# Split GELU times gate: tile 0 in one piece, the last tile in its own input buffer

## The chip, the cores and the metric

The kernel runs on one core of a Trainium2 chip. The metric is the device time of one execution in microseconds (us). The engines that matter here are ScalarE (ACT in the profile), VectorE (DVE), SyncE (SP, which here only issues transfers and waits) and the core's 16 DMA engines. ACTq and SPq are the queues in which ACT and SP hand over transfers; the DMA queues that serve them are q10 (ACT) and q1 (SP).

## The reference

The input x is 32 x 512 x 2048 in float32, that is 16,384 rows of 2048 numbers, 134.2 MB. The output has 16,384 rows of 1024 numbers, 67.1 MB.

```python
x1, x2 = x[..., :1024], x[..., 1024:]
out = 0.5 * x1 * (1 + erf(x1 / sqrt(2))) * x2
```

## The kernel before

The rows are cut into 16 tiles. A tile has 128 partitions with R = 8 rows each: 64 KB per partition come in (8.39 MB a tile) and 32 KB go out (4.19 MB). Tile i uses the input buffer x_bufs[i % 2] and the output buffer o_bufs[i % 2], k = i % 2.

For each tile ACT computes the GELU of the first half of each row into the output buffer (L87), and DVE multiplies that buffer, in place, by the second half of each row (L95). A middle tile is worked in two pieces, of 5 and 3 rows (128x5120 and 128x3072 elements). The first and the last tile are worked in three pieces, of 2, 2 and 4 rows.

The order is written out by hand with semaphores. gelu_done counts the pieces of ACT for DVE, and mul_done the pieces of DVE for the queues. One semaphore per buffer pair, ready[k], counts both the loads into x_bufs[k] and the stores out of o_bufs[k]; ACT waits for its full count before a tile's first piece, so a tile begins when its own load and the store of two tiles earlier have both landed. DVE has no wait of its own except that for ACT.

- Loads are issued by SP (L49). Tile 0 is loaded in two halves of 4 rows, each with a semaphore of its own (first[0], first[1]), and tile 1 in one transfer; all three are issued at the start. Load i + 2 is issued when the products of tile i are done.
- Stores are issued by ACT (L56) for tiles 0 to 13, one transfer a tile, except that tile 0 is stored in two halves. ACT waits for the products of a tile, issues its store, and only then goes on to the next tile. Stores of tile 14 and of the two halves of tile 15 are issued by SP, with the semaphore tail_stored, for which SP waits at the very end (L125).
- A transfer of 4 KB, the opening, is issued by ACT at the start, into a scrap tile that nothing reads.

Of the kernel before, what the change touches and what calls it, by code (L numbers as in the profile page):

```python
# [1 line left out]

# [4 lines left out]

GELU = mybir.ActivationFunctionType.Gelu


@with_exitstack
def kernel(
    ctx: ExitStack,
    tc: tile.TileContext,
    x: bass.AP,
    out: bass.AP,
):
    nc = tc.nc
    P = nc.NUM_PARTITIONS

    x_flat = x.flatten_outer_dims()
    out_flat = out.flatten_outer_dims()
    n_rows, dim = x_flat.shape
    half = dim // 2

    R = 8
    x_t = x_flat.rearrange("(n p r) d -> n p r d", p=P, r=R)
    o_t = out_flat.rearrange("(n p r) d -> n p r d", p=P, r=R)
    n_tiles = x_t.shape[0]
    x_bufs = [nc.alloc_sbuf_tensor(f"x{k}_tile", [P, R, dim], x.dtype) for k in range(2)]  # L30
    o_bufs = [nc.alloc_sbuf_tensor(f"o{k}_tile", [P, R, half], out.dtype) for k in range(2)]

    first = [nc.alloc_semaphore(f"first{j}") for j in range(2)]
    ready = [nc.alloc_semaphore(f"ready{k}") for k in range(2)]
    gelu_done = nc.alloc_semaphore("gelu_done")
    mul_done = nc.alloc_semaphore("mul_done")
    tail_stored = nc.alloc_semaphore("tail_stored")
    opened = nc.alloc_semaphore("opened")  # L40
    scrap = nc.alloc_sbuf_tensor("scrap_tile", [8, 128], x.dtype)
    n = {sem.name: 0 for sem in [*first, *ready, gelu_done, mul_done, tail_stored, opened]}

    def counted(ins, sem, by):
        ins.then_inc(sem, by)
        n[sem.name] += by

    def load(i, rows, sem):
        ins = nc.sync.dma_start(out=x_bufs[i % 2][:, rows, :], in_=x_t[i][:, rows, :])  # L49
        counted(ins, sem, 16)  # L50
        return ins

    def store(queue, i, rows, sem):
        queue.wait_ge(mul_done, n[mul_done.name])
        counted(
            queue.dma_start(out=o_t[i][:, rows, :], in_=o_bufs[i % 2][:, rows, :]), sem, 16  # L56
        )

    opening = nc.scalar.dma_start(out=scrap[:, :], in_=x_t[0][:8, 0, :128])
    counted(opening, opened, 16)
    for ins in (
        opening,
        load(0, slice(0, 4), first[0]),
        load(0, slice(4, 8), first[1]),
        load(1, slice(0, 8), ready[1]),
    ):  # L70
        tc.no_tile_sem_insts.add(ins.ins.name)
    tc.close()
    tc.compile()  # L73

    for i in range(n_tiles):
        k = i % 2
        last = i == n_tiles - 1
        pieces = i == 0 or last
        steps = ((0, 2), (2, 4), (4, 8)) if pieces else ((0, 5), (5, 8))
        for lo, hi in steps:  # L80
            rows = slice(lo, hi)
            if i == 0 and lo % 4 == 0:
                nc.scalar.wait_ge(first[lo // 4], 16)
            elif lo == 0:
                nc.scalar.wait_ge(ready[k], n[ready[k].name])
            counted(
                nc.scalar.activation(  # L87
                    out=o_bufs[k][:, rows, :], in_=x_bufs[k][:, rows, :half], func=GELU
                ),
                gelu_done,  # L90
                1,
            )
            nc.vector.wait_ge(gelu_done, n[gelu_done.name])
            counted(
                nc.vector.tensor_mul(  # L95
                    out=o_bufs[k][:, rows, :],
                    in0=o_bufs[k][:, rows, :],
                    in1=x_bufs[k][:, rows, half:],
                ),
                mul_done,  # L100
                1,
            )
            if pieces and hi % 4 == 0:
                if last:
                    store(nc.sync, i, slice(hi - 4, hi), tail_stored)
                else:
                    store(nc.scalar, i, slice(hi - 4, hi), ready[k])
        if not pieces:
            if i == n_tiles - 2:
                store(nc.sync, i, slice(0, R), tail_stored)  # L110
            else:
                store(nc.scalar, i, slice(0, R), ready[k])
        if i + 2 < n_tiles:
            nc.sync.wait_ge(mul_done, n[mul_done.name])
            load(i + 2, slice(0, R), ready[k])


    nc.scalar.wait_ge(opened, 16)
    nc.scalar.drain()  # L119
    for sem in (*first, *ready, opened):  # L120
        nc.scalar.sem_clear(sem)
    nc.vector.drain()
    nc.vector.sem_clear(gelu_done)
    nc.sync.sem_clear(mul_done)
    nc.sync.wait_ge(tail_stored, n[tail_stored.name]).then_inc(  # L125
        tail_stored, -n[tail_stored.name]
    )


# [1 line left out]
_INS = ['x']  # L131
_OUTS = [((32, 512, 1024), 'float32')]


# [23 lines left out]
```

## Time and profile before

| What | Value |
|---|---|
| Median of 3 timed runs | 469.32 us (469.19 to 469.43) |
| Span of the profiled execution | 467.8 us; its own device time isn't listed apart from this span |
| DVE busy | 140.5 us (30%), 34 instructions |
| ACT busy | 115.5 us (25%), 35 instructions |
| ACT waiting for stores to land | 301.8 us, 14 times, 21.9 us at most |
| ACT waiting for loads to land | 35.6 us, 3 times |
| DVE waiting for ACT | 319.7 us, 18 times |
| SP's queue waiting for DVE, ahead of loads | 396.5 us, 14 times |
| q1 (SP's transfers) | 2880 packets, 142.61 MB, 70.6% of 16 engines' time |
| q10 (ACT's transfers) | 2176 packets, 58.73 MB, 29.1% |
| A load, hand-over to landing | 44.4 us (median) |
| A full store, hand-over to landing | 44.7 us (median) |

The span goes from the first to the last instruction of the execution. Busy shares are those of an engine over the span; the share of a DMA queue is the time that its packets took, over the time of 16 engines. A stretch of the span can show a DMA share a little over 1.00, because a packet is counted where it starts. A packet here is one run of contiguous bytes in a partition: 64 KB for a whole load, 32 KB for half a load or a whole store, 16 KB for half a store.

### The profile page before, as it was taken

What the parts mean: (1) busy time and instruction counts of PE and PEld (TensorE: products, weight loads), DVE (VectorE), ACT (ScalarE), POOL (GpSimd) and SP (SyncE); (2) the same over time, 40 slices, a digit from 0 to 9 for tenths busy, and PEclk for the clock granted to TensorE, in tenths of its full rate; (3) what the DMA queues carried; (4) which work ended last, traced back from release to release, by engine and by line L of the source; (5) the groups of instructions that cost most, each with busy time, mean ns of one, the idle gap of its engine ahead of it and who ended that gap; (6) DMA issues with size and microseconds to landing.
All of it is one profiled execution on the core that took longest, in us unless ns stands there. A gap on an engine that the chain in (4) does not pass through costs nothing.

```text
span 467.8 us, 154 instructions
## 1 busy us (share of the span) xinstructions
DVE 140.5 (30%) x34; ACT 115.5 (25%) x35; POOL 0.2 (0%) x4
## 2 busy tenths in 40 slices
DVE  0330515207051060511606115060150702507043
ACT  1320606041060410604105050050501506014060
POOL 0000000000000000000000000000000000000000
DMA  8999999999999999999999999999999999999988
GB/s 359 448 448 448 398 406 496 403 403 448 459 437 403 440 412 493 403 403 448 487 409 403 445 406 493 403 403 448 493 403 403 448 426 471 403 426 426 493 384 379
DMA packets 5057, 201.34 MB, mean 430 GB/s; under 512 B 568, under 2 KB 576, under 8 KB 576
## 3 DMA queue, kind: packets, MB, share of 16 engines
q1 hardware_dynamic: 2880, 142.61, 70.6%
q10 hardware_dynamic: 2176, 58.73, 29.1%
q14 instruction: 1, 0.01, 0.0%
HBM read 134.22 MB, written 67.11 MB: 430 GB/s over the span
## 4 chain that ended last, share of the span: by engine, by line
DMA 76%; DVE 14%; ACT 8%; ACTq 0%; SPq 0%; issue 0%
DMA out_dram<-o_tile 66%; DVE o_tile L95 14%; DMA x_tile<-in_x_dram 10%; ACT o_tile L87 8%; ACTq L119 0%; SPq L49 0%
## 5 line engine op out<-in xcount | busy, mean ns | idle before, releaser
L95 DVE TENSOR_TENSOR o_tile<-o_tile,x_tile 128x5120 f32<-128x5120 f32 (+3 forms) x34 | 140.5, 4171 | 319.7 <-ACT o_tile L87 319.7
L87 ACT ACTIVATE o_tile<-x_tile 128x5120 f32<-128x5120 f32 (+3 forms) x34 | 114.3, 3407 | 337.3 <-DMA out_dram<-o_tile 301.8
L87 ACT ACT_TABLE_LOAD x1 | 1.3, 1283 | 2.9 <-PEq L73 2.9
L142 POOL MEMSET const-bfloat16-1.0<- 128x1 bf16 x1 | 0.1, 102 | 0.0
L142 POOL MEMSET const-uint8-127<- 128x1 uint8 x1 | 0.1, 101 | 0.0
L142 POOL MEMSET const-float32-0.0<- 128x1 f32 x1 | 0.1, 99 | 0.2 <-issue 0.2
L142 POOL MEMSET const-float32-1.0<- 128x1 f32 x1 | 0.1, 98 | 0.0
## 6 DMA issues: line engine op xcount, KB each, us to landing
out_dram<-o_tile ACTq DMA_DIRECT2D x13, 4096.0 KB, 44.7
x_tile<-in_x_dram SPq DMA_DIRECT2D x2, 4096.0 KB, 16.7
out_dram<-o_tile ACTq DMA_DIRECT2D x2, 2048.0 KB, 34.4
out_dram<-o_tile SPq DMA_DIRECT2D x1, 4096.0 KB, 25.2
out_dram<-o_tile SPq DMA_DIRECT2D x2, 2048.0 KB, 7.8
x_tile<-in_x_dram SPq DMA_DIRECT2D x15, 44.4
scrap_tile<-in_x_dram ACTq DMA_DIRECT2D x1, 4.0 KB
```

Source lines behind the costliest of these rows:

```text
L87: nc.scalar.activation(out=o_bufs[k][:, rows, :], in_=x_bufs[k][:, rows, :half], func=GELU),
L95: nc.vector.tensor_mul(out=o_bufs[k][:, rows, :], in0=o_bufs[k][:, rows, :], in1=x_bufs[k][:, rows, half:],),
L142: nc = _bacc.Bacc("TRN2", target_bir_lowering=False, num_devices=1)
```

## The change

- **Tile 0** is loaded by one transfer with ready[0], worked in two pieces of 5 and 3 rows like the middle tiles, and stored by one transfer. The semaphores first[0] and first[1] are gone, and with them two clears at the end.
- **Tile 15** (the last) no longer uses an output buffer. ACT writes the GELU over the first half of each row in the input buffer. DVE writes the product into the front of the same buffer, packed: row r of the product lies at elements 1024 r to 1024 r + 1023 of each partition. A piece's product thus covers space that an earlier piece has read, and DVE now waits for its own earlier product (mul_done) before each of the three pieces. The two stores of tile 15 read from there, again 16 KB per partition each.
- **Store 13** counts on tail_stored and no longer on ready[1], so that ACT begins tile 15 when load 15 has landed.
- In the program text the load of tile i + 2 now stands ahead of the store of tile i. They are issued by different engines, and the order of instructions on each engine is otherwise the same.

```diff
-    def load(i, rows, sem):
-        ins = nc.sync.dma_start(out=x_bufs[i % 2][:, rows, :], in_=x_t[i][:, rows, :])
-        counted(ins, sem, 16)
+    def load(i):
+        ins = nc.sync.dma_start(out=x_bufs[i % 2][:, :, :], in_=x_t[i])
+        counted(ins, ready[i % 2], 16)
...
-        load(0, slice(0, 4), first[0]),
-        load(0, slice(4, 8), first[1]),
-        load(1, slice(0, 8), ready[1]),
+        load(0),
+        load(1),
...
+    packed = x_bufs[(n_tiles - 1) % 2][:, :, :].rearrange("p r d -> p (r d)")
+    packed = packed[:, : R * half].rearrange("p (r d) -> p r d", d=half)
     for i in range(n_tiles):
         k = i % 2
+        x_buf = x_bufs[k]
         last = i == n_tiles - 1
-        pieces = i == 0 or last
-        steps = ((0, 2), (2, 4), (4, 8)) if pieces else ((0, 5), (5, 8))
-        for lo, hi in steps:
+        made = packed if last else o_bufs[k][:, :, :]
+        for lo, hi in ((0, 2), (2, 4), (4, 8)) if last else ((0, 5), (5, 8)):
             rows = slice(lo, hi)
-            if i == 0 and lo % 4 == 0:
-                nc.scalar.wait_ge(first[lo // 4], 16)
-            elif lo == 0:
+            if lo == 0:
                 nc.scalar.wait_ge(ready[k], n[ready[k].name])
+            gelu = x_buf[:, rows, :half] if last else made[:, rows, :]
             counted(
-                nc.scalar.activation(
-                    out=o_bufs[k][:, rows, :], in_=x_bufs[k][:, rows, :half], func=GELU
-                ),
+                nc.scalar.activation(out=gelu, in_=x_buf[:, rows, :half], func=GELU),
                 gelu_done,
                 1,
             )
+            if last:
+                nc.vector.wait_ge(mul_done, n[mul_done.name])
             nc.vector.wait_ge(gelu_done, n[gelu_done.name])
             counted(
                 nc.vector.tensor_mul(
-                    out=o_bufs[k][:, rows, :],
-                    in0=o_bufs[k][:, rows, :],
-                    in1=x_bufs[k][:, rows, half:],
+                    out=made[:, rows, :], in0=gelu, in1=x_buf[:, rows, half:]
                 ),
                 mul_done,
                 1,
             )
-            if pieces and hi % 4 == 0:
-                if last:
-                    store(nc.sync, i, slice(hi - 4, hi), tail_stored)
-                else:
-                    store(nc.scalar, i, slice(hi - 4, hi), ready[k])
...
+            if last and hi % 4 == 0:
+                store(nc.sync, i, slice(hi - 4, hi), made, tail_stored)
         if i + 2 < n_tiles:
             nc.sync.wait_ge(mul_done, n[mul_done.name])
-            load(i + 2, slice(0, R), ready[k])
+            load(i + 2)
+        if i < n_tiles - 3:
+            store(nc.scalar, i, slice(0, R), made, ready[k])
+        elif i == n_tiles - 3:
+            store(nc.scalar, i, slice(0, R), made, tail_stored)
+        elif i == n_tiles - 2:
+            store(nc.sync, i, slice(0, R), made, tail_stored)
```

More of the change, by code (lines that the diff above doesn't have):

```diff
@@ L31 @@
     o_bufs = [nc.alloc_sbuf_tensor(f"o{k}_tile", [P, R, half], out.dtype) for k in range(2)]
-    first = [nc.alloc_semaphore(f"first{j}") for j in range(2)]
     ready = [nc.alloc_semaphore(f"ready{k}") for k in range(2)]
@@ L41 @@
     scrap = nc.alloc_sbuf_tensor("scrap_tile", [8, 128], x.dtype)
-    n = {sem.name: 0 for sem in [*first, *ready, gelu_done, mul_done, tail_stored, opened]}
+    n = {sem.name: 0 for sem in [*ready, gelu_done, mul_done, tail_stored, opened]}
     def counted(ins, sem, by):
@@ L46, in counted, with store @@
         n[sem.name] += by
-    def load(i, rows, sem):
-        ins = nc.sync.dma_start(out=x_bufs[i % 2][:, rows, :], in_=x_t[i][:, rows, :])
-        counted(ins, sem, 16)
+    def load(i):
+        ins = nc.sync.dma_start(out=x_bufs[i % 2][:, :, :], in_=x_t[i])
+        counted(ins, ready[i % 2], 16)
         return ins
-    def store(queue, i, rows, sem):
+    def store(queue, i, rows, from_, sem):
         queue.wait_ge(mul_done, n[mul_done.name])
-        counted(
-            queue.dma_start(out=o_t[i][:, rows, :], in_=o_bufs[i % 2][:, rows, :]), sem, 16
-        )
+        counted(queue.dma_start(out=o_t[i][:, rows, :], in_=from_[:, rows, :]), sem, 16)
     opening = nc.scalar.dma_start(out=scrap[:, :], in_=x_t[0][:8, 0, :128])
@@ L102 @@
             )
-            if pieces and hi % 4 == 0:
-                if last:
-                    store(nc.sync, i, slice(hi - 4, hi), tail_stored)
-                else:
-                    store(nc.scalar, i, slice(hi - 4, hi), ready[k])
[L108 to L112, printed above, removed]
+            if last and hi % 4 == 0:
+                store(nc.sync, i, slice(hi - 4, hi), made, tail_stored)
         if i + 2 < n_tiles:
             nc.sync.wait_ge(mul_done, n[mul_done.name])
-            load(i + 2, slice(0, R), ready[k])
+            load(i + 2)
[5 more added lines that the diff above has]
+            store(nc.sync, i, slice(0, R), made, tail_stored)
     nc.scalar.wait_ge(opened, 16)
     nc.scalar.drain()
-    for sem in (*first, *ready, opened):
+    for sem in (*ready, opened):
         nc.scalar.sem_clear(sem)
```

## The prediction

> **What bounds the kernel now.** First the page's DMA rows (mean busy share of the 16 engines in fortieths of the span, then what they moved):
>
> ```profile
> span 467.8 us, 154 instructions
> DVE 140.5 (30%) x34; ACT 115.5 (25%) x35; POOL 0.2 (0%) x4
> DMA  8999999999999999999999999999999999999988
> HBM read 134.22 MB, written 67.11 MB: 430 GB/s over the span
> ```
>
> DVE and ACT are idle for 70 and 75%; the DMA engines never are. Then the table by stretch (length, DVE, ACT and POOL busy, clock, DMA share, GB/s); two tiles take 58 us:
>
> ```profile
> 58.00:116.00 58.00, 19.80 (x5) 14.25 (x4) 0.00 (x0) 1.00 1.01 435
> 116.00:174.00 58.00, 17.52 (x4) 14.24 (x4) 0.00 (x0) 1.00 1.00 434
> 348.00:406.00 58.00, 17.52 (x4) 14.25 (x4) 0.00 (x0) 1.00 1.00 434
> ```
>
> Share 1.00 and 434 GB/s in every stretch: the middle is bound by bytes, 25.17 MB a pair of tiles, and the change leaves the bytes alone. So only the two ends are left, and whether a queue runs dry there. Third, the chain of waits that ended last (start, length, what), its head and its tail:
>
> ```profile
> 0.73 0.38 SPq L49
> 1.16 0.42 SPq L49
> 1.64 45.36 DMA x_tile<-in_x_dram
> 47.02 4.48 ACT o_tile L87
> ...
> 403.75 44.74 DMA out_dram<-o_tile
> 448.51 1.91 ACT o_tile L87
> 450.42 1.80 ACTq L119
> 452.22 3.52 ACT o_tile L87
> 455.76 4.42 DVE o_tile L95
> ```
>
> The chain names engines and waits, but that is only the order of release; 44.7 us for a 4 MB store, which alone would need 9.7, is queueing. Fourth, the timeline of the first tiles, for when data lands and when transfers are handed over:
>
> ```profile
> 12.79 3.71 ACT L87 ACTIVATE o_tile<-x_tile 128x2048 f32<-128x2048 f32 x2 [8.65 <-DMA x_tile<-in_x_dram]
> 22.47 3.62 ACT L87 ACTIVATE o_tile<-x_tile 128x4096 f32<-128x4096 f32 x1 [5.97 <-DMA x_tile<-in_x_dram]
> 30.58 0.36 ACTq L56 DMA_DIRECT2D out_dram<-o_tile  x1
> 71.40 7.12 ACT L87 ACTIVATE o_tile<-x_tile 128x5120 f32<-128x5120 f32 x2 [17.26 <-DMA out_dram<-o_tile]
> ```
>
> Last, the packet records. In 1 us windows each engine starts one packet on the queue, and the share gives its length: 121.3% is 1.213 us for 32 KB, 241.9% is 2.418 us for 64 KB, 61.1% is 0.611 us for 16 KB:
>
> ```profile
> q1 hardware_dynamic: 16, 0.52, 121.3%
> ...
> q1 hardware_dynamic: 16, 1.05, 241.9%
> ...
> q10 hardware_dynamic: 16, 0.26, 61.1%
> ```
>
> Per engine the kernel before is 15 loads x 8 packets x 2.418 + 16 x 1.213 (tile 0's halves) = 309.57, and stores 14 x 8 x 1.213 + 32 x 0.611 (tiles 0 and 15) = 155.41: 464.98 us. The first packet starts at 1.74; the first sixteen take 1.81 in place of 1.21 (225.9% of 0.8 us), so 0.59 more; from the last packet's end (467.37) to the wake of SP's last wait, 0.44. Together 467.75 of 467.84. **There is about 0.1 us of idle time to win in the whole span.** The median, 469.32, lies 1.48 above this span, which I carry over.
>
> **The change, part by part.**
>
> *Tile 0 as one load.* Halves landed at 12.79 and 22.47, 9.68 apart, and 4.194 MB at 434 GB/s is 9.66: the second half gets its full rate, so one load of both lands at about 22.45. Tile 0's work then starts 9.7 us later; in steady tiles load to last product is 60.31 - 47.02 = 13.3, so store 0 (ACT's queue) and load 2 (SP's queue) are handed over at 35.8, in place of 30.58 for the last ones. Cover: load 1, already queued, keeps the engines busy from 21.7 for 8 x 2.418, to 41.0. That leaves 5.2 us from hand-over to first packet. Rows: 1.0 us at the start (0.73 to 1.74, empty queue), 5.1 for the store handed over at 19.26, whose first packet starts at 24.36; but that one stood behind load packets of engines that never paused. I take the near end, since a ring that runs empty resembles the start; at the far end it just fits. Cost 0; without that cover, 1 us a us. In packets, 16 x 1.213 become 8 x 2.418: -0.06. The slow first wave: still 0.59 as a latency (taken), 0 at best, or, if it scales with packet size, 1.2: -0.6 to +0.6.
>
> *Tile 0 as one store.* 16 x 0.611 become 8 x 1.213: -0.07. It starts when load 1 has at most one packet per engine left, not at 24.4, so load 1 runs undiluted: tile 1 should start at 41.5 to 43 in place of 47.02. That lead isn't kept: by tile 2's start loads 0 to 2 and store 0 must have moved, the same 29.4 MB, and one or two packets of store 1 with them, so it starts at 71.4 to 73. From then on the two queues alternate packet for packet, 8 x (2.418 + 1.213) = 29.05 a tile, with the store one or two rounds ahead of the load: ACT will wait for loads, not stores. Both queues always hold some 15 us of work when a tile's products finish.
>
> *Waiting for no store.* Tile 15 needs only load 15, not store 13. Landing times of those two are 44.4 us (median load) and 44.74 after the same hand-over, so the wait is worth 0.35 us, and under cover: with all loads and stores 0 to 13 moved, 16 + 8 + 8 packets of stores 14 and 15 are always left, 19.5 us. If store 13 is ahead, load 15's last packets run alone and land at the same 448.1 to 448.5. Nothing off the end; store 14 follows on the same queue as before.
>
> *Tile 15 in its own buffer.* The three activations write strided rows in place, and the products read two strided operands. Activations: 1.90, 1.90, 3.61 us in rows with as many elements; products 2.29, 2.29, 4.42. The nearest rows for a strided operand are these products, whose second operand already steps by 2048. (5493 - 3351) ns / 2048 elements is 1.05 ns an element whatever the shape, so I take no change. DVE gains a wait on its own last product. The first two products took 4.49 together against 2 x 2.29, so they overlapped by 0.09; a wait for another engine's result shows 0.02 to 0.03 after it. Cost 0.1 per wait, on the first store's path; the third product stood idle 0.81 for ACT, so it absorbs this. The Trainium skill, "VectorE: DVE Perf Modes", section "The DRAIN you can't avoid", says that a semaphore costs nothing extra, since the next operation waits for an empty pipe anyway; by it the sum has 0 for 0.1, and neither reaches the end.
>
> Queued behind these waits is only the tail on SP: the stores were handed over at 454.97 and 460.2, and their packets start at 457.2 and 462.07 with no gap before them. By the 1.0 us of the start, 1.2 and 0.8 us of cover are left, at worst almost none. The wait takes 0.1 of the first. Two semaphore clears fewer on ACT lie under the last store.
>
> **Sum.** 467.84 - 0.06 - 0.07 = 467.7, + 1.48 = 469.2 us. Bounds: the first wave, -0.6 and +0.6, gives 468.6 to 469.8; up to 0.3 us of lost cover at the tail takes it to 470.1.
>
> **Rivals.**
>
> *The tail runs dry (slower).* If reading and writing one buffer makes products slower, the last store comes late. Three products back to back from 450.45 are 9.0 us; more than 0.2% is lost when the last hand-over passes 462.07 - 1.01 + 0.94 = 462.0, that is from 1.28 times their present length on. At 1.5 times, the last store is handed over at 464.0, its packets start at 465.0 and the end comes 2.9 us later: 472.1. For: cover of 0.8 us or less is the thinnest in the kernel. Against: product length follows element count in all four shapes. 0.07.
>
> *The head runs dry (slower).* If the hand-over of load 2 needs more than 5.2 us, all engines pause at 41.0. With 7 us, 471.0. Against: no row is over 5.1. 0.02.
>
> *Each transfer carries a cost of its own (faster).* Two transfers fewer; a lone one, from hand-over to wake, took 12.79 - 0.73 - 9.66 = 2.4 us more than its bytes, so 469.3 - 4.8 = 464.5. Against: halves queued together landed 9.68 apart, 0.02 over their bytes. 0.03. The Trainium skill, "DMA: Bandwidth & Descriptors", section "Anatomy of one DMA — SWDGE (gpsimd) path", gives such a fixed cost, 2.0 us plus bytes by 436 GB/s, for transfers issued by GpSimd; taken for these, an estimate of 465.3. The trace shows that cost once, at the start, and hidden after it.
>
> *The change does not do what it says:* its no-wait clause removes 0.35 us that nothing was paying for. That is part of the forecast, not against it.
>
> **Numbers.** Forecast 0.88, at 469.2; slower rivals 0.07 and 0.02; faster 0.03. 0.2%, about what a measurement of this kernel can tell from no change, is 0.94 us: 468.4 to 470.3 counts as the same, which holds the forecast's whole range. 468.6 to 470.1 leaves out only rivals and the outermost bounds.
>
> **What would show it.** Right: DMA share 1.00 and 434 GB/s in each 58 us; tile 1 starting at 41.5 to 43 and tile 2 at 71.4 to 73; ACT's large wait now on x_tile loads; stores landing 36 to 42 us after hand-over in place of 44.7; tile 15 starting within 0.6 of 448.5, and the last store's landing about 7.5 us after its hand-over. Wrong: a stretch before 60 us or after 448 with a DMA share well below that of before, products of tile 15 longer than 2.29 and 4.42, or 64 KB packets not at 2.42.

## The result, and the profile after

The changed kernel takes 470.17 us (median of 15 runs, 469.96 to 470.93) against 469.30 us (15 runs, 469.13 to 469.44): ratio 1.0019, 95% interval 1.0012 to 1.0027. It is slower by 0.87 us, 0.19%, just inside the 0.2% that the prediction called the same, but clear of 1 by its interval, and above the range's upper end of 470.1.

The page of the profiled execution, which took 470.19 us:

```profile
span 468.6 us, 151 instructions
DMA  8999999999999998999999999999999999999998
HBM read 134.22 MB, written 67.11 MB: 430 GB/s over the span
```

Bytes and rate look as before; 0.7 us of 468 does not show here. The table by stretch (length, DVE, ACT and POOL busy, clock, DMA share, GB/s) does show it:

```profile
36.00:42.00 6.00, 0.00 (x0) 0.00 (x0) 0.00 (x0) 1.00 0.99 350
58.00:116.00 58.00, 17.52 (x4) 14.25 (x4) 0.00 (x0) 1.00 1.00 434
```

and the first of these stretches in the kernel before:

```profile
36.00:42.00 6.00, 0.00 (x0) 0.00 (x0) 0.00 (x0) 1.00 1.01 437
```

The DMA share after the change is 0.99 between 36 and 42 us, and yet only 350 GB/s are moved, where the kernel before moves 437: the packets there are slow, not missing. The packet records of the changed kernel for two windows of 1 us (q1, in which each of the 16 engines starts one 64 KB load packet, so that the share is their mean length):

```profile
q1 hardware_dynamic: 16, 1.05, 243.5%
...
q1 hardware_dynamic: 16, 1.05, 350.6%
```

From 36.2 us the packets take 2.44 us, from 38.5 us 3.51 us; the store queue's first packets follow at 42.06. The matching window of the kernel before, ahead of its first store packets (from 21.5 us; the 32 packets are 16 loads and 16 short semaphore writes, which take next to nothing):

```profile
q1 hardware_dynamic: 32, 1.05, 267.3%
```

There they take 2.67 us. In units of all engines, that is the excess over 2.42 us added up and divided by 16, the stall ahead of the first store is **1.09 us after the change and 0.24 us before it**.

The chain of waits after the change (start, length, what), its head and tail:

```profile
1.17 43.28 DMA x_tile<-in_x_dram
44.47 4.48 ACT o_tile L84
...
405.74 43.35 DMA x_tile<-in_x_dram
449.11 1.91 ACT x_tile L84
...
456.36 0.02 DVEq L90
456.43 4.42 DVE x_tile L92
```

The tail has the length of before: 449.11 to the last product's end, 11.7 us, against 448.51 and 11.7. It merely starts 0.6 us later. DVE's wait for itself is the entry of 0.02 us.

The account by packet records, end of the last packet 468.19 against 467.37, is +0.82: the first stall +0.85; smaller slow packets of before between 24 and 40 us, gone, -0.12; the first wave of loads 0.70 in place of 0.60, +0.10; fewer and larger packets -0.14; engines spread wider at the end, about +0.1. These add up to +0.79. The last landing follows the last packet by 0.34 us in place of 0.44.

### The profile page after: what moved, and what is told of

Same layout as the page of the kernel before. It is cut to its first block, busy times and chain, and to the rows that moved or that the text cites. A ratio compares the mean times of both kernels' runs of the same rounds, so it can differ in the third digit from the quotient of the medians.

```text
span 468.6 us, 151 instructions
## 1 busy us (share of the span) xinstructions
DVE 140.4 (30%) x33; ACT 115.3 (25%) x34; POOL 0.2 (0%) x4
## 4 chain that ended last, share of the span: by engine, by line
DMA 76%; DVE 14%; ACT 8%; ACTq 0%; issue 0%; SPq 0%; DVEq 0%
DMA out_dram<-o_tile 57%; DMA x_tile<-in_x_dram 18%; DVE o_tile L92 13%; ACT o_tile L84 7%; ACT x_tile L84 1%; DVE x_tile L92 1%; ACTq L112 0%; SPq L48 0%; DVEq L90 0%
## 5 line engine op out<-in xcount | busy, mean ns | idle before, releaser
L92 DVE TENSOR_TENSOR o_tile<-o_tile,x_tile 128x5120 f32<-128x5120 f32 (+1 forms) x30 | 131.4, 4421 | 303.3 <-ACT o_tile L84 303.3
L84 ACT ACTIVATE o_tile<-x_tile 128x5120 f32<-128x5120 f32 (+1 forms) x30 | 106.8, 3608 | 318.1 <-DMA out_dram<-o_tile 284.4
L92 DVE TENSOR_TENSOR x_tile<-x_tile 128x2048 f32<-128x2048 f32 (+1 forms) x3 | 9.0, 3002 | 17.1 <-ACT x_tile L84 17.1
L84 ACT ACTIVATE x_tile<-x_tile 128x2048 f32<-128x2048 f32 (+1 forms) x3 | 7.2, 2468 | 20.5 <-DMA x_tile<-in_x_dram 20.5
## 6 DMA issues: line engine op xcount, KB each, us to landing
out_dram<-o_tile ACTq DMA_DIRECT2D x14, 4096.0 KB, 44.7
```

The source lines that it names most:

```text
L84: nc.scalar.activation(out=gelu, in_=x_buf[:, rows, :half], func=GELU),
L92: nc.vector.tensor_mul(out=made[:, rows, :], in0=gelu, in1=x_buf[:, rows, half:]),
```

## The experiments

A stall in the text is the excess just described, from the one profiled execution of each kernel, which can be a faster or slower one than the median. Differences of a tenth or two between stalls mean little: three kernels with the same head as before (before, e2, e9) show 0.24, 0.13 and 0.30 us at their first store, and three with the same first store as after (after, e1, e8) 1.09, 1.07 and 1.15. All times are medians, beside 469.25 to 469.36 us for the kernel before, run beside them on the same chip.

### Head or tail

**One half of the change each.** e1 keeps the new head and restores the old tail; e2 is the reverse.

```diff
# e1, against the kernel after
-        made = packed if last else o_bufs[k][:, :, :]
+        made = o_bufs[k][:, :, :]
...
-            if last:
-                nc.vector.wait_ge(mul_done, n[mul_done.name])
...
-        if i < n_tiles - 3:
+        if i < n_tiles - 2:
             store(nc.scalar, i, slice(0, R), made, ready[k])
...
# e2, against the kernel after
...
-        load(0),
+        load(0, slice(0, 4), first[0]),
+        load(0, slice(4, 8), first[1]),
...
+            if i == 0 and hi % 4 == 0:
+                store(nc.scalar, i, slice(hi - 4, hi), made, ready[k])
...
```

> Tile 0 as after the change (one load, one store), the last tile and store 13 as before it. Theory A (the queue runs dry when load 1 ends, because load 2 and store 0 are handed over at 35.9) and theory B (a one-off cost of the first store, wherever it falls): both put the loss at the head, so 470.2 us, ratio 1.002, with the last packet of load 1 at about 3.4 us in place of 2.42. Theory C (the tail in its own buffer costs the time): 469.3, ratio 1.000.

> Tile 0 as before the change (two halves, three pieces, two stores), the last tile in its own buffer and store 13 on the other semaphore. Theories A and B: 469.3 us, ratio 1.000, DMA packets of 20 to 36 us as before. Theory C: 470.2, ratio 1.002.

e1: 470.29 us, ratio 1.0017 (1.0004 to 1.0030), stall 1.07 us at 38.65. e2: 469.27 us, ratio 0.9998 (0.9989 to 1.0007), stall 0.13 us at 21.67. The loss is the head's. The tail in its own buffer, with its waits, costs and gains nothing beyond 0.1%.

The profiled execution of e2 took 469.85 us, 0.58 above its median, and its trace shows where (window from 84.7 us):

```profile
q1 hardware_dynamic: 16, 1.05, 298.9%
```

That is a second stall, 0.57 us, on load packets that start at 85.0. Four of store 1's eight packets on each engine were still to come, so no queue was starting. Slow packets on all engines are therefore not always the start of a store; what made these is open.

### A dry queue?

First store packet 6.1 us after its hand-over, load 1 due to end at 41.0, and a cover of 5.2 us: this looked like the dry head that the prediction had as a rival. Hand-over was moved both ways, by the pieces of tile 0 alone.

```diff
# e3: in place of ((0, 5), (5, 8)) for tile 0
+        for lo, hi in ((0, 2), (2, 4), (4, 8)) if last else ((0, 8),) if i == 0 else ((0, 5), (5, 8)):
# e4
+        for lo, hi in ((0, 2), (2, 4), (4, 8)) if last else ((0, 2), (2, 4), (4, 8)) if i == 0 else ((0, 5), (5, 8)):
```

> The kernel after the change, but tile 0 worked in one piece of 8 rows, so that load 2 and store 0 are handed over at about 38.4 in place of 35.9, 2.4 us later. Theory A: load 1 still ends at 41.0 and each us of lateness costs a us: 470.2 + 2.4 = 472.6, ratio 1.007, first store packets at 44.5 to 45.2. Theory B: hand-over still ahead of 41.0, the one-off cost unchanged: 470.2, ratio 1.002.

> The kernel after the change, but tile 0 worked in three pieces of 2, 2 and 4 rows, so that its last product ends at about 34.5 in place of 35.9, 1.4 us earlier. Theory A: hand-over to first packet is 6.1 us, so the packets are there at 40.6, before load 1 ends: the gap of about 1.0 us closes and the time is 469.2, ratio 1.000. Theory B: the one-off cost stays: 470.2, ratio 1.002.

e3, handed over at 38.45: 469.92 us, ratio 1.0012 (1.0003 to 1.0021). e4, at 34.37: 470.53 us, ratio 1.0024 (1.0010 to 1.0038). Later was not 2.4 us slower, earlier not faster: the dry queue (theory A) falls. The packet records of e3, windows from 38.5 and from 41 us:

```profile
q1 hardware_dynamic: 16, 1.05, 243.9%
...
q1 hardware_dynamic: 32, 1.05, 345.6%
```

Load 1's last packets (38.5) are normal here. The slow ones, 3.45 us, are load 2's first, which started at 41.07: load 2 had arrived 2.6 us after its hand-over, with no gap. In e4 the slow packets start at 36.3, 3.03 us long:

```profile
q1 hardware_dynamic: 16, 1.05, 302.8%
```

The stall moves with the hand-over, over packets that have nothing to do with a load's end. (e4's stall of 0.61 us belongs to its fastest execution, 470.00 us; the median is 0.53 above that.)

### The load or the store?

e5 has one load and two stores of tile 0, e6 two loads and one store. e7 writes 64 KB to the output before store 0, e8 only widens the opening transfer to 128 partitions.

```diff
# e5, against the kernel after
...
+            if i == 0 and hi % 4 == 0:
+                store(nc.scalar, i, slice(hi - 4, hi), made, ready[k])
...
# e6, against e2
-            if i == 0 and hi % 4 == 0:
-                store(nc.scalar, i, slice(hi - 4, hi), made, ready[k])
...
# e8, against the kernel after
...
-    opening = nc.scalar.dma_start(out=scrap[:, :], in_=x_t[0][:8, 0, :128])
+    opening = nc.scalar.dma_start(out=scrap[:, :], in_=x_t[0][:, 0, :128])
# e7, against e8
+    nc.scalar.wait_ge(opened, 16)
+    counted(nc.scalar.dma_start(out=o_t[0][:, 0, :128], in_=scrap[:, :]), opened, 16)
...
+        if i == 0:
+            nc.scalar.wait_ge(opened, 32)
...
```

> The kernel after the change, with tile 0 worked in three pieces and stored in two halves of 2 MB as before the change; one load stays. Theory B (the first store of a run stalls the packets in flight once, and a 4 MB store handed over together with a load more than a 2 MB store by itself): slow load packets shortly ahead of the first store packet add 0.2 to 0.3 us, as before the change, in place of 1.1: 469.3 to 469.5 us. Theory D (the loss comes of the load in one piece): 470.2.

> The tail as after the change; tile 0 loaded in two halves and worked in three pieces as before, but stored by one transfer of 4 MB, handed over at about 30.6 together with load 2. Theory B: the stall is about 1 us, 470.1 us. Theory D: 469.3.

> The kernel after the change, with the opening transfer over 128 partitions (64 KB) and, as soon as it has landed, 64 KB stored from there into tile 0's part of the output, which store 0 later overwrites (ACT waits for that first). Theory B in the form that the first write to the output memory costs about 1 us once: the slow packets of 38.6 us are gone; if the cost is hidden beside the slow start of the loads 469.2 us, if it only moves to about 6 us, 470.2 with slow packets there. Theory B in the form that each first large store stalls: slow packets at 38.6 as before, 470.2.

> The kernel after the change, with only the opening transfer over 128 partitions in place of 8, so that ACT's queue has been used on all 16 DMA engines before store 0, but nothing written to the output. If the stall is that of a queue's first use on an engine: slow packets of 38.6 gone, 469.2 us. If it is that of the first write to the output memory or of a large store: 470.2.

e6: 469.88 us, ratio 1.0020 (1.0012 to 1.0029), with 1.09 us of stall at 33.8, 3.2 us after the hand-over at 30.64. Its window from 33.5 us:

```profile
q1 hardware_dynamic: 16, 1.05, 350.9%
```

So the store in one piece brings the stall without the load in one piece. e5 did not come out as either theory had it: 474.49 us, ratio 1.0118 (1.0088 to 1.0149), two stalls (0.45 us at 31.3, 0.52 at 41.0) and then engines that drift apart, until load 15 lands on the first engine at 446.1 and on the last at 452.1 us. Tile 15 waits for the last of them and begins at 452.08 in place of 449.11. That drift isn't explained. Its second stall came 3.3 us after the second half store had been handed over, at a time when the first half's packets were still moving, so the queue wasn't empty.

e7: 470.29 us, ratio 1.0022 (1.0013 to 1.0030). Its opening was itself caught between load packets and landed at 22.9, and the 64 KB written then, in packets of 512 bytes, landed only at 44.6, so store 0 left at 44.64. The stall, 0.74 us, came at 46.2, after those 64 KB had gone to the output. Their own start slowed no load packet: from 20 to 46 us all took 2.42 us. e8: 470.33 us, ratio 1.0026 (1.0015 to 1.0037), stall 1.15 us at 38.7. Neither a first use of ACT's queue over all 128 partitions nor the first write to the output is the cause.

### Once, or at each start of the store queue?

e9 is the kernel before with store 6 on SP, so that ACT's queue runs out in mid-run and starts again with store 7. e11 is the kernel after without store 0.

```diff
# e9, against the kernel before
+            elif i == 6:
+                store(nc.sync, i, slice(0, R), ready[k])
# e11, against the kernel after (store 0 left out)
+        if i == 0:
+            continue
         if i < n_tiles - 3:
```

> The kernel before the change, with store 6 issued by SP ahead of load 8, so that ACT's DMA queue runs empty in mid-run and starts again with store 7 in 32 KB packets. Theory E (each time that the store queue starts from empty, all engines lose about one store packet's time, 1.0 to 1.2 us for 32 KB): slow load packets some 3 us after the hand-over of store 7, 470.3 us, ratio 1.002. Theory F (the cost comes once, with the first store of a run, whatever follows): 469.3 us, no slow packets there.

> The kernel after the change without store 0, so tile 0's part of the output isn't written, and the time is shorter by its bytes, 9.7 us. If the stall at 38.6 comes of the store: no slow packets there, but 1.0 to 1.2 us of them some 3 us after store 1 is handed over (about 56 us), 460.5 us. If it comes of the hand-over of load 2: slow packets at 38.6 as before, none at store 1, 460.5 us.

e11: 460.42 us. The packet records from 38.5 us and from 57.8 us:

```profile
q1 hardware_dynamic: 16, 1.05, 242.0%
...
q1 hardware_dynamic: 16, 1.05, 362.3%
```

Load 2 was handed over alone at 35.99 and nothing was slow. Store 1 became the first store, handed over at 55.32, and the packets from 57.9 took 3.62 us: 1.2 us of stall. **The stall is the store's.** e9: 471.45 us, ratio 1.0046 (1.0034 to 1.0058). Its records from 232.5 us (load packets, 15 of 16 in the window, so 3.36 us each):

```profile
q1 hardware_dynamic: 15, 0.98, 314.9%
```

Store 7 was handed over at 229.90, and 3 us later all engines lost 0.88 us, in mid-run, with everything long in use: the cost comes again with a new start of the store queue from empty, not once. The whole run is 1.1 us slower than theory E's 470.3. It lost another 0.5 us at 224, where the last store packets in SP's queue take 1.56 us in place of 1.21 and load 8 follows them, and the engines ended 1.6 us apart; these may be most of the rest of 2.1 us. What it is not: in the kernel after, q10 has no packet between 66.95 (end of store 0's) and 71.06 (start of store 1's), and nothing is slow at 71.06. Store 1 had been handed over at 57.76, while store 0 was still moving. So a pause of 4 us in the queue's packets brings no stall by itself. A longer pause of all writes, 8.6 us, goes along with the start in e9, and no run tells the two apart there. Nor is a start the only thing that slows load packets: e2 at 85.0 (0.57 us), e5 at 41.0 (0.52 us), e10 at 31.3 (0.19 us, 4.6 us ahead of any hand-over) and e17 at 82.6 (0.27 us) have slow load packets while no store queue starts.

### What sets its size

Two small first packets were tried, e10 in the kernel after and e12 in the kernel before.

```diff
+            parts = (
+                (slice(0, 16), slice(0, 1)),
+                (slice(0, 16), slice(1, R)),
+                (slice(16, P), slice(0, R)),
+            )
+        for p, r in parts:
+            counted(queue.dma_start(out=o_t[i][p, r, :], in_=from_[p, r, :]), sem, 16)
# e12: the same, rows 0:1, 1:4 and 0:4, for the first half store
```

> The kernel after the change, with store 0 handed over in three parts: row 0 of partitions 0 to 15 (one packet of 4 KB per engine), rows 1 to 7 of these (28 KB), and the other 112 partitions whole (32 KB). Theory E1 (the cost is that of the first store packet alone): slow packets add 0.1 to 0.2 us in place of 1.1, 469.3 us. Theory E2 (the cost comes with the first large packets, whatever ran ahead of them): slow packets as after the change, 470.2 us.

> The kernel before the change, with the first half store of tile 0 handed over in three parts: row 0 of partitions 0 to 15 (4 KB packets, one per engine), rows 1 to 3 of these (12 KB), and the other 112 partitions (16 KB). Theory E1: the slow packets of 21.7 us (0.24 us) go, 469.0 to 469.1 us, faster than both kernels. Theory E2 or F: 469.3 us.

Both miss their purpose: 480.97 us (ratio 1.0245, 1.0232 to 1.0258) and 472.56 us (1.0076, 1.0063 to 1.0090). In e10 the rate fell to 423 GB/s over 58 to 116 us and the engines ended 2.7 us apart, so something in this cut, by partitions and into three transfers, has a price of its own that hides the question in the times. In the traces the start does cost less with a small first packet, as theory E1 had it: in e10 the packets that start at 38.9 us take 2.60 us, a stall of 0.18 us, and in e12 the slow wave at 21.7 is gone. But in e12 0.26 us at 32.0 and 0.52 us at 41.5 took its place.

Then the hand-overs of load and store were parted (e13), and the store's packets cut by rows alone (e14, e15).

```diff
# e13, against the kernel after
+        if i == 0:
+            nc.scalar.wait_ge(mul_done, n[mul_done.name])
+            counted(nc.scalar.activation(out=o_bufs[1][:, 0:4, :],
+                    in_=o_bufs[0][:, 0:4, :], func=GELU), pause, 1)
+            nc.scalar.wait_ge(pause, 1)
# e14, against e6: for tile 0
+            store(nc.scalar, i, slice(0, 4), made, ready[k])
+            store(nc.scalar, i, slice(4, R), made, ready[k])
# e15, against the kernel before: loads and stores of rows 0:2 and 2:8 for tile 0
```

> The kernel after the change, with one more activation (4096 elements into the idle output buffer, 3.6 us) on ACT ahead of store 0, so that load 2 is handed over alone at 35.9 and store 0 alone at about 39.6. Theory G (the stall is large because a load and a store are handed over together): slow packets of 0.2 to 0.5 us, 469.4 to 469.7 us. Theory H (it goes by the store's packet size, 32 KB against 16 KB): 1.0 to 1.2 us of slow packets, now some 3 us behind 39.6 and none at 38.6, 470.0 to 470.3 us.

> As the run with two loads and one store, but store 0 in two halves (16 KB packets) that are handed over one behind the other at 30.6, together with load 2. Theory G: slow packets of about 1.0 us ahead of the first store packet. Theory H: 0.25 to 0.5 us. The time is over 471 us in both, if it was the store queue's late start with 16 packets per engine in front of it, and not the load in one piece, that made the run with one load and two stores slow (stores land behind loads there, so that tiles wait for stores).

> The kernel before the change, with tile 0 loaded and stored as rows 0 to 1 and rows 2 to 7 in place of two halves of 4 rows (store packets of 8 and 24 KB; pieces of 2, 3 and 3 rows). Theory H: the stall at the first store falls from 0.24 to about 0.12 us, 469.1 to 469.2 us, the only version so far that could be ahead of both kernels. Theory G, or a second stall at the larger packets: 469.3 us or more.

e13: 469.98 us, ratio 1.0030 (1.0010 to 1.0050). Its windows from 38.5 and from 41 us:

```profile
q1 hardware_dynamic: 16, 1.05, 243.1%
...
q1 hardware_dynamic: 32, 1.05, 324.5%
```

Load 2 alone at 35.93 slows nothing; store 0 alone at 39.58 makes 0.82 us, less than the 1.0 to 1.2 of theory H and well above the 0.2 to 0.5 of theory G. The hand-over together (theory G) falls. Two of e13's twelve runs took 474.0 and 474.3 us, and no trace shows why. e14: 470.18 us, ratio 1.0034 (1.0019 to 1.0049). Its window from 33.5 us:

```profile
q1 hardware_dynamic: 16, 1.05, 265.2%
```

With 16 KB packets, handed over together with load 2, the first stall is 0.23 us, the size of before. But a second one of 0.55 us follows at 40.1, on load 1's last packets, and the forecast of more than 471 us failed for the median: six of eleven runs took 469.6 to 470.2 us, the profiled one among them, and five 471.6 to 472.8. e15: 469.54 us, ratio 1.0005 (0.9997 to 1.0014): stalls of 0.10, 0.25 and 0.28 us, no gain. No version that does all the work beat the kernel before.

Last, store 0 of the kernel after was cut by rows with nothing else changed: two transfers of 16 KB packets (e16), four of 8 KB (e17).

```diff
+        if i == 0:
+            for lo in range(0, R, 4):  # e17: 2 in place of 4
+                store(nc.scalar, i, slice(lo, lo + 4), made, ready[k])
```

> The kernel after the change, with store 0 handed over at 35.9 as two halves of 4 rows one behind the other (16 KB packets, 16 per engine) in place of one transfer (32 KB, 8 per engine). Theory H (the stall at the start of the store queue goes by the store's packet size): the packets of load 1 that start at 38.6 take 2.6 to 2.9 us in place of 3.5. Rival (the stall does not depend on it): 3.5 us as after the change. A second stall of about 0.5 us near 41 to 44 may follow, as in the two runs with 16 KB packets, and the time is 469.5 to 470.5 us.

> As the run with two halves, but store 0 in four transfers of 2 rows (8 KB packets, 32 per engine), 1.6 us of hand-over in place of 0.4. Theory H: the first slow packets of load 1 take 2.45 to 2.7 us. Rival: 3.5 us. The time is open: with 32 packets per engine the stores of tile 0 land late, and tile 2 waits for them, so 471 us or more.

The windows from 38.5 us, first of e16, then of e17:

```profile
q1 hardware_dynamic: 16, 1.05, 327.8%
```

```profile
q1 hardware_dynamic: 16, 1.05, 274.5%
```

3.51 us with 32 KB, 3.28 with 16 KB, 2.75 with 8 KB: smaller packets do give a smaller stall (1.09, 0.86, 0.32 us), but less so than theory H said (2.6 to 2.9 and 2.45 to 2.7 us), and 16 KB here costs nearly four times what it costs in e14 and in the kernel before. Packet size takes part and isn't the whole of it. **What else sets the size stays open.** The stalls of 16 KB starts run from 0.13 to 0.86 us, those of 32 KB from 0.61 (e4) to 1.2 us. For 32 KB the traces give a hint: where the slow packets started 1.5 to 1.9 us after the hand-over (e13, e7, e4) they lost 0.61 to 0.82 us, and where they started 2.6 to 3.2 us after it 0.88 to 1.20. No run was made to test it.

Both kernels are some 6 us slower for another reason: 476.83 us (ratio 1.0151, 1.0126 to 1.0176) and 476.53 us (1.0154, 1.0137 to 1.0171). One packet of each queue is served in turn, so 16 or 32 small packets in front hold back store 0 until load 2 and load 3 have gone by; tile 2 then waits for store 0 until 88.96 and 91.10 us, load 4 is handed over only at 102 to 104, and SP's queue is empty meanwhile. A stretch of e17:

```profile
90.00:104.00 14.00, 8.40 (x2) 7.12 (x2) 0.00 (x0) 1.00 0.71 308
```

The first load packets after that pause were slow as well, by 1.08 and 1.43 us; both queues started from empty there, so the traces don't say which of them it was.

## Why the prediction was wrong, point by point

- **What bounds it: right.** 434 GB/s in every 58 us, before and after. It named the two ends as the only places left; the loss lies in one of them.
- **Tile 0 as one load: right in its times, and no cost of its own shows.** Tile 0 landed at 22.62 (forecast 22.45), hand-over at 35.94 (35.8). e6 has the stall with two loads, as large (1.09 us) and at much the same price (ratio 1.0020 against e1's 1.0017), so the load in one piece doesn't bring it.
- **Tile 0 as one store: the step that failed.** The prediction priced this as -0.07 us of packets and nothing else. It had no term for the start of the store queue, which the trace of before showed: 2.67 us packets at 21.5 in place of 2.42. The sum's 467.75 of 467.84 seemed to leave nothing over, since it laid the packets end to end at their recorded lengths, and these records overlap a little (load packets of 2.418 us follow each other every 2.414 us), by about as much as the omitted 0.24 us and some smaller slow packets. The omitted term is 0.24 us before and 1.09 after, in e1 1.07 and in e6 1.09: +0.85 us where the sum had -0.07. The range allowed 0.6 us for the first wave and 0.3 for the tail, and nothing for this. Its own sign of being wrong, "64 KB packets not at 2.42", is the one that came. That the store's start brings the stall is shown (e3, e4, e11, e13); why it is larger for one store than for two is shown only in part.
- **Dry head: forecast right, cost 0.** The cover of 5.2 us held: e3, with 2.6 us from hand-over to load 2's first packet, had none to spare and still no gap. The 5.1 us row that was taken as its far bound held 0.24 us of the stall itself.
- **First wave: right.** 0.70 against 0.59, within the 0.6 allowed either way; over the runs it lies between 0.43 and 0.77, with no clear order by packet size.
- **Waiting for no store: right, worth nothing.** Store 13, now alone on its semaphore, landed 41.0 us after hand-over (forecast 36 to 42) and load 15 after 43.3, so tile 15 would have waited for the load anyway. It began at 449.11, 0.6 later than before. ACT's wait in the other tiles is still put down to stores by the profile, against the forecast that it would name loads; both count on one semaphore there, and packet records show store 0's last packet ending at 66.95 and load 2's at 71.78. The order forecast was right, the name that the profile would give was not. The 44.7 us that the page of the profile still gives for a full store comes of the same: store 12 and load 14 were handed over at 376.8, and their last packets ended at 414.95 and 419.78.
- **Tile 15 in its own buffer: right.** Products 2.29 and 4.42 us as forecast, the first two together 4.62 in place of 4.49 (+0.13 against a forecast of 0.1). The first store was handed over at 455.77, 6.66 us after the tile's start against 6.46, and no packet waited for it. That agrees with the row, not with the sentence of the Trainium skill ("VectorE: DVE Perf Modes", "The DRAIN you can't avoid") that a semaphore costs nothing extra; the difference is hidden here.
- **Tile 1 and tile 2** began at 44.47 and 73.55, forecast 41.5 to 43 and 71.4 to 73. Tile 2 is late by the stall. Without it tile 1 would still be 0.4 us past the range: load 1's last data packet ended at 42.78, but its short semaphore writes came behind store 0's first packets, at 43.3 to 44.0.
- **Rivals.** The dry tail and the dry head did not come; e16 and e17 show what a dry queue looks like, a share of 0.71. A fixed cost of each transfer did not come either: with two transfers fewer the account above has a gain of 0.14 us, which is packets. None of the four was the mechanism that occurred.

## What to carry to other kernels

Where the DMA engines never pause, look at how long their packets take, not only at whether they are busy: a share near 1.00 with fewer GB/s is a stall that busy time hides. A store queue that starts from empty beside a running load queue cost all engines up to 1.2 us here, so price its start by the nearest start in the trace, and ask what the change does to that start. With one packet of each queue served in turn, the number of packets sets how two queues share the engines: cutting a transfer into more of them sends it to the back (e16, e17). One profiled execution can hold a stall of its own (e2), so set its time beside the median before a cause is read from it.

## What the runs showed of the hardware that was not expected

- Handing a store of 32 KB packets to an empty queue slows one load packet on each of the 16 engines, which starts 1.5 to 3.2 us later, by 0.6 to 1.2 us; with 8 or 16 KB packets it was 0.1 to 0.9 us, with 512-byte packets (e7) nothing that shows. A load handed over to a queue that still held a load slowed nothing (e11, e13).
- Loads alone (a 64 KB packet on each of 16 engines every 2.414 us, so 434 GB/s) and loads mixed with stores ran at the same 434 GB/s, but a kernel whose first store was cut at partition 16 went on with 423 GB/s over 58 to 116 us (e10); why is open.
- Run-to-run scatter: 0.3 us over 15 runs before, 1.0 us over 15 runs after, 5.3 us over 6 runs of e5. But of the kernel before, too, five of 29 runs beside e1 to e4 took 471.5 to 471.7 us, 2.3 us above the rest; no trace of such a run was kept.
